# Split queries and keys of the attention: DMAs moved from GpSimd's software queue to SyncE's hardware queue

## The chip, the cores and the metric

One core of a Trainium2 chip runs the whole program. The metric is the device time of one execution in microseconds (us). The engines are TensorE (PE, with its weight loads as PEld), VectorE (DVE), ScalarE (ACT), GpSimd (POOL) and SyncE (SP), which only issues DMAs. Each engine takes its instructions in one fixed order; an instruction that waits holds all that stand behind it on its engine. A DMA issued by SP goes into the hardware queue (q1 in the profile), one issued by POOL into the software queue (q0); the data of both move through the core's 16 DMA engines.

## The reference

Two layers of a transformer-like block work on 1024 latent and 256 context tokens of width 1024. In each layer a normed and modulated input is projected into four mixers of 256 columns each: an mLSTM in both directions, a differential attention, a multiscale pool, and a gated convolution. Their outputs go together through one projection with a residual, and then through a SwiGLU feed forward with a residual. The attention has 4 heads, each with two maps of head width 32:

```
q = rms_norm(aq.reshape(B, L, 4, 2, 32), q_norm_g);  k = rms_norm(ak..., k_norm_g)
q, k = apply_axial_rope(q), apply_axial_rope(k)        # latent tokens only
s = einsum('bqhmd,bkhmd->bhmqk', q, k) * 32 ** -0.5;   p = softmax(s)
a = p[:, :, 0] - lam * p[:, :, 1];                     o = einsum('bhqk,bkhe->bqhe', a, v)
```

Latent queries see all 1280 keys, context queries the 256 context keys. The second layer needs no context output. All is float32; the gains are large, so products are made nearly exact by splitting the operands.

## The kernel before

Activations lie with features on partitions and tokens along the free dimension. A dense product is made of three float32r products, of the high and low parts of both operands (`mm3`, lines 274 to 279). Weights come as 256 KB tiles by SP (`load_w`, line 267), ACT copies out the high part and DVE or POOL subtracts the low part; there are two buffers for the raw tile (`wor`, `wfr` and so on in the profile) and five each for high and low.

A layer runs so: projections for mLSTM, convolution and pool; the mLSTM's states; then chunk after chunk of the mLSTM's outputs, with the projections of the attention's queries and keys, of its values, and the steps of the convolution's norm put between them as a filling (`background`); then the attention; the output projection (`out_proj`); the feed forward (`ffn`).

The queries and keys pass through DRAM. `qk_in` (lines 914 to 940) norms and rotates one projected tile of 128 features (4 maps of 32) by up to 512 tokens, writes its high part (ACT, into the buffer `qr`) and its low part (POOL, into `qsq`), and stores both in the scratch `qks`, laid out as [kind, map, high or low, 32 rows, 1280 tokens] (lines 939 and 940). `stacks(h)` (lines 1132 to 1145) loads them for one head: for each of its two maps, a tile `Qs` whose rows 0 to 63 hold the high part twice and rows 64 to 127 the low part twice (two DMAs of 64 rows), and a tile `Ks` with the high and low part, twice over (one DMA of 128 rows). The doubling is the leading [0, 2] of the source's access pattern (`dup`, lines 1126 and 1127), so that one product with 128 rows makes all four partial products. A head's six DMAs are Qs, Qs, Ks, Qs, Qs, Ks. In layer 0 a row has 1280 floats (320 KB a `Qs` DMA, 640 KB a `Ks` DMA); in layer 1 a `Qs` row has 1024 (256 KB). `stacks(0)` stands before the first score tile, and `stacks(1)`, `(2)`, `(3)` two slots after the start of the first, second and third head's scores; a slot is one score tile. The values come by SP from another scratch (`V`, line 1144).

The order on each engine is made by a planner ahead of the run, from a simulated time, from the order of the text as priority, and from free buffers. Only PE, ACT and DVE are held to the order of the text, and only inside the attention (`ordered`, class `Engine`). A DMA of either queue has one of eight semaphores for that queue in turn, so the ninth waits until the first has landed. A buffer is reused when the last one that reads it is done; for a store that is its landing. The tiles `T` (520 columns, 11 buffers) hold among others `yct` and `so` (outputs of convolution and mLSTM on their way to the scratch `ys`, lines 1109 and 911), `so` as loaded from the scratch `os` (line 904), `csq`, `qr` and `qsq`. The tiles `S` (28 buffers) hold `Qs`, `Ks`, the activations and the large work arrays.

In `out_proj` each weight's low part is ordered behind the last DMA of `stacks(3)` in the plan (`self.stack`, lines 1140 and 1332; `after`, lines 229 to 232, which orders without a wait). `woh` on ACT and `wol` on POOL thus stand inside the attention's last head.

Of the kernel before, what the change touches and what calls it, by code (L numbers as in the profile page):

```python
# [11 lines left out]
F32 = mybir.dt.float32  # L12
F32R = mybir.dt.float32r
BF16 = mybir.dt.bfloat16
AF = mybir.ActivationFunctionType
# [3 lines left out]
P = 128  # L19
# [21 lines left out]
# parameter columns of one layer  # L41
# [112 lines left out]
class Engine:  # L154
    """an engine whose instructions keep the order they are written in while builder.ordered is set"""
# [28 lines left out]
class Builder:  # L184
# [24 lines left out]
    # PSUM banks of each phase: for the dense products, for all else  # L209
# [19 lines left out]
    def after(self, ins, gate):  # L229
        """order ins behind gate in the schedule, without a wait"""  # L230
        self.tc.add_manual_dep(ins.ins, gate.ins.name, mybir.DependencyInfo(
            mybir.DependencyClass.NoSync, mybir.DependencyReason.DATA), reason="load order")
# [5 lines left out]
    def cb(self, name, n):  # L238
        """a constant column repeated n times"""
        return self.c(name)[:, 0:1].to_broadcast([P, n])  # L240
# [21 lines left out]
    def load_w(self, ap, n, eng=None, nm="w", gate=None):  # L262
        """weights [P, n] from DRAM as an exact sum of two float32r tiles"""
        hi = self.wp.tile([P, 544], F32R, tag="wh", name=f"{nm}h", bufs=5)
        lo = self.wp.tile([P, 544], F32R, tag="wl", name=f"{nm}l", bufs=5)
        raw = self.wp.tile([P, 544], F32, tag="wr", name=f"{nm}r", bufs=2)
        self.load = self.nc.sync.dma_start(raw[:, :n], ap)
        self.copy(hi[:, :n], raw[:, :n])
        ins = self.sub_lo(lo[:, :n], raw[:, :n], hi[:, :n], eng)
        if gate is not None:  # L270
            self.after(ins, gate)
        return hi, lo
# [12 lines left out]
    def rsqrt_steps(self, y, ms, eps, l=None):  # L285
        """y = (ms + eps) ** -0.5 with l for scratch; ms may be in PSUM"""
        nc = self.nc
        n = y.shape[-1]
        if l is None:
            l = self.T("rsl")[:, :n] if n > 64 else self.Q("rslq", n)  # L290
        epsc = self.eps[eps]
        nc.scalar.activation(l, ms, AF.Ln, bias=epsc)
        nc.scalar.activation(y, l, AF.Exp, scale=-0.5)
        yield
        nc.vector.scalar_tensor_tensor(l, ms, epsc, y, ALU.add, ALU.mult)
        nc.vector.scalar_tensor_tensor(l, l, -0.5, y, ALU.mult, ALU.mult)
        nc.vector.scalar_tensor_tensor(y, l, 1.5, y, ALU.add, ALU.mult)

    def sigmoid(self, out, x, n, t=None):
        """exp(min(x, 0) - log(1 + exp(-|x|))) with t for scratch"""  # L300
        nc = self.nc
        t = self.T("sgm")[:, :n] if t is None else t
        for _ in self.sigmoid_steps(out, x, t):
            pass
# [12 lines left out]
    def setup(self):  # L317
# [22 lines left out]
        # silu of the conditioning vectors, split  # L340
# [11 lines left out]
        # lambda of each layer  # L352
# [29 lines left out]
    def mod_steps(self, l, quads):  # L382
        """columns of (lat, ctx) modulation; each group of four 512 chunks runs on four column tiles"""
# [29 lines left out]
    def mod_vec(self, l):  # L413
        """all columns of (lat, ctx) modulation, two 512 chunks at a time: products and sums over the tiles of c on
        the vector engine, sums over partitions on the tensor engine; in steps of one vector instruction"""
# [32 lines left out]
    def norm_r(self, h, c0, n):  # L448
        """1 / rms of every token, on all partitions"""
        nc = self.nc  # L450
        px = self.PX("nps")
        for k in range(KT):
            sq = self.T("nsq")
            v = h[k][:, c0:c0 + n]
            nc.scalar.activation(sq[:, :n], v, AF.Square)
            g = slice((k % 4) * 32, (k % 4) * 32 + 32)
            nc.tensor.matmul(px[g, :n], self.cb("one", 32), sq[:, :n], start=(k < 4), stop=(k >= 4))
            if k == KT // 2 - 1:
                yield
        sm = self.T("nsum")[:, :n]  # L460
        self.copy(sm, px[:, :n])
        px = self.PX("nps2")
        nc.tensor.matmul(px[:, :n], self.cb("comb", P), sm, start=True, stop=True)
        r = self.T("nrstd")[:, :n]
        self.rsqrt(r, px[:, :n], 1e-6, sm)
        return r
# [8 lines left out]
    def norm_in(self, h, chunks):  # L475
        """the first norm: normalised in place, before the modulation is there"""
# [6 lines left out]
    def norm_mod(self, l, gname, sh, sc):  # L483
        """the split tiles of u, and what fills a chunk of them from h"""
# [39 lines left out]
    def fm_gen(self, l, idx, u, chunks, consume, src="w_fm", eng=None):  # L524
        """one 128 column tile, features on partitions"""
# [17 lines left out]
    def tm_gen(self, aps, n, u, cs, consume, w=None):  # L543
        """n columns, tokens on partitions"""
# [16 lines left out]
    def mixers(self, l, u, norm):  # L561
        """norm: what is left of the norm, in steps"""
# [7 lines left out]
        self.oc = range(0 if need else 2, NCH)      # token chunks whose outputs are needed  # L570
# [7 lines left out]
        # mLSTM: v with a ones column, gates  # L578
# [115 lines left out]
    def mix(self, a, n, b):  # L694
        """n steps of a, then steps of a and b in turn"""
# [10 lines left out]
    def mlstm_rows(self, Z):  # L706
# [11 lines left out]
        # log sigmoid of the forget gates  # L718
# [34 lines left out]
        nc.vector.tensor_scalar(mp[:, 1:2], am[:, 0:1], mp[:, 0:1], -1.0, ALU.max, ALU.mult)   # -Glast  # L753
        nc.scalar.activation(mp[:, 2:3], mp[:, 1:2], AF.Exp, bias=mp[:, 0:1])                  # e_old
# [19 lines left out]
        # -max(m, running max) of every row, spread block diagonally over the heads, as an exact sum of two  # L774
# [58 lines left out]
    def mlstm_chunk(self, c, kT, qT, Cst):  # L833
        """stages of the outputs of one chunk"""
# [79 lines left out]
    def qk_in(self, kind, i, c0, n, ps):  # L914
# [24 lines left out]
        nc.gpsimd.dma_start(self.qk_scr[kind, 4 * i:4 * i + 4, 0, :, c0:c0 + n], hi)  # L939
        nc.gpsimd.dma_start(self.qk_scr[kind, 4 * i:4 * i + 4, 1, :, c0:c0 + n], lo)  # L940
# [21 lines left out]
    def pool(self, u, i):  # L962
# [14 lines left out]
        for (o, c0, n) in segs:  # L977
            g = nc.gpsimd.tensor_tensor
            b = o + 8                       # column of token 0
            sw = s[:, o:o + n + 16]  # L980
            uw = up[:, o:o + n + 16]
            # column j of sw/uw is token j - 8
            if i == 0:
                g(sw[:, 7:n + 10], uw[:, 6:n + 9], uw[:, 7:n + 10], ALU.add)            # windows of 2
                x = self.S("psx")
                g(x[64:P, 8:n + 8], sw[64:P, 7:n + 7], sw[64:P, 9:n + 9], ALU.add)      # windows of 4
                res = ((0, 64, s, b), (64, P, x, 8))
            else:
                x = self.S("psx")
                g(sw[:, 1:n + 16], uw[:, 0:n + 15], uw[:, 1:n + 16], ALU.add)           # 2  # L990
                g(x[:, 2:n + 15], sw[:, 1:n + 14], sw[:, 3:n + 16], ALU.add)            # 4
                g(sw[:, 4:n + 13], x[:, 2:n + 11], x[:, 6:n + 15], ALU.add)             # 8
                g(x[64:P, 8:n + 8], sw[64:P, 4:n + 4], sw[64:P, 12:n + 12], ALU.add)    # 16
# [23 lines left out]
    def conv_in(self, u, i, cy):  # L1017
        """gated inputs: ctx tokens at column 0, latent tokens at column 271, zeros between"""
# [16 lines left out]
    def conv_taps(self, cy, acc):  # L1035
        """one tap of each half at a time, the middle one first"""
# [17 lines left out]
    def conv(self, acc):  # L1054
        """layer norm, silu and pointwise product, in steps; what is left of the last ones goes into the attention"""
# [64 lines left out]
    def attention(self):  # L1120
# [3 lines left out]
        gd = nc.gpsimd.dma_start  # L1124
# [7 lines left out]
        def stacks(h):  # L1132
            Qs, Ks = [], []
            for m in range(2):
                mp = 2 * h + m
                Qm = self.S(f"Qs{m}", F32R)
                gd(Qm[0:64, q0:NT], dup(self.qk_scr[0, mp, 0, :, q0:NT]))
                gd(Qm[64:P, q0:NT], dup(self.qk_scr[0, mp, 1, :, q0:NT]))
                Km = self.S(f"Ks{m}", F32R)
                self.stack = gd(Km[:, 0:NT], dup(self.qk_scr[1, mp].rearrange("a r n -> (a r) n")))  # L1140
# [6 lines left out]
        def scores(h, b0, nk, at):  # L1147
            """exp of both maps combined, unscaled: p0 - (lam * L0 / L1) * p1; two steps for each score tile"""
# [23 lines left out]
        def shared():  # L1172
            """one bank for both uses of a slot"""
# [15 lines left out]
        def weights_t(at, nk, aT):  # L1189
            """the combined weights with keys on partitions; a step for each two key tiles"""  # L1190
# [19 lines left out]
        def values(h, b0, nk, aT):  # L1210
            """the two query blocks on two column tiles; two steps of products, then the move out of PSUM"""
# [15 lines left out]
        def subln(pair, b0):  # L1227
            """norm over each head, with tokens on partitions for the statistics; the sums of the first map undo
            the missing scale of eps"""
# [32 lines left out]
        # four slots of a score tile each for a unit; its transposes and products some slots later  # L1262
# [4 lines left out]
        for i, (h, b0, nk) in enumerate(units):  # L1267
# [9 lines left out]
            d = {1: 4, 2: 1}.get(left, 0)        # the last ones earlier  # L1277
# [8 lines left out]
        rest = {1: 2, 2: 1, 3: 1, 4: 2, 5: 2}      # steps of what is left of the convolution, by slot  # L1286
# [174 lines left out]
def _layout(x, c, ctx, c_ctx, norm1_g, norm2_g, mod_w, mod_b, w_in, mlstm_gate_b, mlstm_norm_g,  # L1461
# [31 lines left out]
    # [l, chunk, k pair, 128, 2 k, 512]  # L1493
    o["mod_w"] = mod_w.reshape(L, 4, 2, P, 12, 512).transpose(0, 4, 1, 3, 2, 5).reshape(L, 12, 4, P, 1024)
    order = [(0, 256), (256, 512), (1040, 1296), (1296, 1552), (1808, 2064), (2064, 2320), (2320, 2576)]
    fm = np.concatenate([w_in[:, :, s:e] for s, e in order], axis=2)         # 14 tiles
    # [l, tile, piece, 128, 4 k, 128]
# [44 lines left out]
```

## Time and profile before

| | us |
|---|---|
| three timed runs | 3360.95, 3363.9, 3366.14 (median 3363.9) |
| profiled execution, span from first to last instruction | 3361.6 |
| PE busy in the span | 3099.8 (92%) |
| DVE, ACT, POOL busy | 1805.3, 1130.7, 520.9 |
| attention of layer 0, first score product to the fourth head's last units | 572 to about 790 |
| attention of layer 1 | about 2320 to 2500 |

PE is busy nearly everywhere but in the two attentions and just ahead of them; there its busy share falls to 5 to 8 tenths in the slices of the page. POOL's DMA issues stand in its own time line (about 0.7 us each), SP's in that of its queue ("SPq"). In the time line a row is: start, duration, engine, line, operation, what it writes and reads, shape, count, and in brackets the idle time of the engine before it and what ended it.

### The profile page before, as it was taken

The page shows a single profiled execution, that of the slowest core. Times are in us where ns is not written, and L with a number is a line of the kernel's source. Part 1 is how long each engine was busy: PE and PEld are TensorE (multiplying, and loading weights), DVE is VectorE, ACT ScalarE, POOL GpSimd, SP SyncE. Part 2 cuts the span into 40 slices and gives each one's busy share as a digit, 9 for nine tenths or more (in the row PEclk, how much of TensorE's full clock was granted, in tenths as well). Part 3 has the DMA queues.
Part 4 walks back from the last instruction along what each step waited for, and adds up shares of the span by engine and source line. Part 5 has one row for each costly group of instructions (what it writes and reads, how often), then busy time and mean ns, then how long its engine had stood idle before and what let it go on. Part 6 is the DMA issues. An engine that isn't in the chain of part 4 may idle for free. (4 is left out here: it accounts for less than half of the span.)

```text
span 3361.6 us, 41928 instructions
## 1 busy us (share of the span) xinstructions
PE 3099.8 (92%) x16504; PEld 2459.5 (73%) x16504; DVE 1805.3 (54%) x2868; ACT 1130.7 (34%) x2233; POOL 520.9 (15%) x412
## 2 busy tenths in 40 slices
PE   7999886778999999999999898985789999999999
PEld 3766664557778888888888686764667788888887
DVE  6494555875365555455433668566873533343343
ACT  4212444766441111111111622444874411111111
POOL 2240321232400000000000333321424000000000
PEclk9999987989999999999999998998999999999999
DMA  7123335223222222222111211344422111111112
GB/s 275 54 68 103 92 90 102 45 49 129 76 70 75 69 79 73 69 71 79 43 38 38 75 45 47 83 98 93 78 92 80 55 44 47 51 48 46 45 54 76
DMA packets 180566, 247.44 MB, mean 74 GB/s; under 512 B 70032, under 2 KB 82192, under 8 KB 180368
## 3 DMA queue, kind: packets, MB, share of 16 engines
q1 hardware_dynamic: 123600, 214.68, 20.3%
q0 software_dynamic: 56768, 30.07, 5.2%
q8 instruction: 130, 2.13, 0.3%
q14 instruction: 68, 0.56, 0.1%
HBM read 214.10 MB, written 30.41 MB: 73 GB/s over the span
## 5 line engine op out<-in xcount | busy, mean ns | idle before, releaser
L164 DVE SCALAR_TENSOR_TENSOR h<-xps,mod,h 128x512 f32<-128x512 f32 (+1 forms) x440 | 302.9, 697 | 187.1 <-PE xps L164 182.7
L164 PE MATMUL fps<-uh,wgh 128*128 128x512 f32 (+1 forms) x880 | 329.6, 375 | 6.1 <-ACT fsg L164 6.1
L164 PE MATMUL fps<-ul,wgh 128*128 128x512 f32 (+1 forms) x880 | 328.5, 373 | 0.6 <-DVE ul L164 0.6
L164 PE MATMUL fps<-uh,wgl 128*128 128x512 f32 (+1 forms) x880 | 328.4, 373 | 0.0
L164 PE MATMUL xps<-gl,wxh 128*128 128x512 f32 (+1 forms) x880 | 327.9, 373 | 0.0
L164 PE MATMUL fps<-uh,wuh 128*128 128x512 f32 (+1 forms) x880 | 327.3, 372 | 0.0
L164 PE MATMUL xps<-gh,wxl 128*128 128x512 f32 (+1 forms) x880 | 327.0, 372 | 0.0
L164 PE MATMUL fps<-uh,wul 128*128 128x512 f32 (+1 forms) x880 | 326.8, 371 | 0.0
L164 PE MATMUL fps<-ul,wuh 128*128 128x512 f32 (+1 forms) x880 | 326.8, 371 | 0.0
L164 PE MATMUL xps<-gh,wxh 128*128 128x512 f32 (+1 forms) x880 | 326.5, 373 | 0.0
L164 DVE TENSOR_TENSOR fsg<-fsg,fps 128x512 f32<-128x512 f32 (+1 forms) x110 | 69.7, 634 | 421.9 <-PE fps L164 419.5
L164 PE MATMUL fmps<-uh,wfh 128*128 128x512 f32 (+1 forms) x592 | 222.8, 376 | 13.7 <-ACT kT L164 13.7
L164 PE MATMUL fmps<-ul,wfh 128*128 128x512 f32 (+1 forms) x592 | 221.3, 374 | 0.0
L164 PE MATMUL fmps<-uh,wfl 128*128 128x512 f32 (+1 forms) x592 | 221.0, 373 | 0.0
L164 DVE TENSOR_REDUCE ls<-sc 128x1 f32<-128x1280 f32 (+1 forms) x144 | 195.0, 1367 | 32.1 <-PE sc L164 31.6
L164 PE MATMUL sc<-Ks,Qs 128*128 128x512 f32 (+1 forms) x400 | 124.4, 419 | 85.6 <-ACT pr L164 83.8
L164 DVE SCALAR_TENSOR_TENSOR acc<-cy,par,acc 128x1286 f32<-128x1286 f32 (+28 forms) x120 | 199.7, 1702 | 1.0
L164 PEld LDWEIGHTS fps<-uh,wgh 128*128 128x128 f32 x880 | 165.9, 189 | 44.7 <-ACT fsg L164 6.3
L164 PEld LDWEIGHTS fps<-ul,wgh 128*128 128x128 f32 x880 | 166.0, 189 | 36.4 <-DVE ul L164 2.6
L164 PEld LDWEIGHTS xps<-gh,wxh 128*128 128x128 f32 x880 | 165.5, 188 | 35.3 <-issue 3.1
L164 PEld LDWEIGHTS xps<-gl,wxh 128*128 128x128 f32 x880 | 165.3, 188 | 34.6 <-DVE gl L164 3.0
L164 PEld LDWEIGHTS fps<-uh,wgl 128*128 128x128 f32 x880 | 166.0, 189 | 32.4 <-issue 1.1
(286 smaller groups left out, 6130.4 us busy)
## 6 DMA issues: line engine op xcount, KB each, us to landing
mw<-in_mod_w SPq DMA_DIRECT2D x160, 256.0 KB, 3.9
wgr<-in_ffn_in SPq DMA_DIRECT2D x88, 256.0 KB, 2.6
wur<-in_ffn_in SPq DMA_DIRECT2D x88, 256.0 KB, 2.6
wxr<-in_ffn_out SPq DMA_DIRECT2D x88, 256.0 KB, 2.6
wor<-in_w_out SPq DMA_DIRECT2D x64, 256.0 KB, 2.7
wfr<-in_w_fm SPq DMA_DIRECT2D x56, 256.0 KB, 2.6
h<-in_xT SPq DMA_DIRECT2D x16, 640.0 KB, 6.8
Ks<-qks POOLq DMA_DIRECT2D x16, 640.0 KB, 26.2
```

The lines of the kernel that those rows point to most:

```text
L164: ins = f(*args, **kw)
```

## The change

The stores of `qk_in` and the loads of `stacks` are issued by SP instead of POOL. Both sides of each are now declared float32 instead of float32r (the same bits). The shapes, the sizes, the number and the order in the text stay. In the listing below only these edits are shown; elsewhere the diff takes out comments and docstrings.

```diff
@@ qk_in
-        nc.gpsimd.dma_start(self.qk_scr[kind, 4 * i:4 * i + 4, 0, :, c0:c0 + n], hi)
-        nc.gpsimd.dma_start(self.qk_scr[kind, 4 * i:4 * i + 4, 1, :, c0:c0 + n], lo)
+        for x, v in enumerate((hi, lo)):
+            nc.sync.dma_start(self.qk_scr[kind, 4 * i:4 * i + 4, x, :, c0:c0 + n].bitcast(F32), v.bitcast(F32))
@@ attention
-        gd = nc.gpsimd.dma_start
+        gd = nc.sync.dma_start
@@ stacks
-                gd(Qm[0:64, q0:NT], dup(self.qk_scr[0, mp, 0, :, q0:NT]))
-                gd(Qm[64:P, q0:NT], dup(self.qk_scr[0, mp, 1, :, q0:NT]))
+                for x in range(2):
+                    gd(Qm[x * 64:x * 64 + 64, q0:NT].bitcast(F32), dup(self.qk_scr[0, mp, x, :, q0:NT].bitcast(F32)))
                 Km = self.S(f"Ks{m}", F32R)
-                self.stack = gd(Km[:, 0:NT], dup(self.qk_scr[1, mp].rearrange("a r n -> (a r) n")))
+                self.stack = gd(Km[:, 0:NT].bitcast(F32),
+                                dup(self.qk_scr[1, mp].rearrange("a r n -> (a r) n").bitcast(F32)))
```

## Rows read from the trace of the kernel before

**Rows 1.** The page's first lines: busy time, share of the span, instructions.

```profile
span 3361.6 us, 41928 instructions
PE 3099.8 (92%) x16504; PEld 2459.5 (73%) x16504; DVE 1805.3 (54%) x2868; ACT 1130.7 (34%) x2233; POOL 520.9 (15%) x412
```

**Rows 2.** DMA issues: names, queue, count, KB each, median us to landing.

```profile
wor<-in_w_out SPq DMA_DIRECT2D x64, 256.0 KB, 2.7
Ks<-qks POOLq DMA_DIRECT2D x16, 640.0 KB, 26.2
Qs<-qks POOLq DMA_DIRECT2D x16, 320.0 KB, 21.9
qks<-qr POOLq DMA_DIRECT2D x16, 256.0 KB, 7.2
...
V<-vs SPq DMA_DIRECT2D x8, 320.0 KB, 2.9
```

**Rows 3.** DMA view, 2325 to 2333 us: GB/s by slice; queue: packets, MB, share of 16 engines.

```profile
GB/s 55 1 55 28 55 52 52 54 54 54 54 54 54 28 52 28 54 52 54 54 54 54 54 54 54 28 52 28 54 52 54 54 54 54 31 45 45 29 27 1
q0 software_dynamic: 67, 0.34, 11.0%
```

**Rows 4.** The same view, 787 to 797 us, where two `yr` loads of 640 KB run.

```profile
DMA packets 820, 3.75 MB, mean 375 GB/s; under 512 B 91, under 2 KB 91, under 8 KB 818
```

**Rows 5.** Time line of the way into layer 0's attention.

```profile
536.91 0.70 POOL L1137 DMA_DIRECT2D Qs<-qks  x1
...
542.48 1.56 SPq L1109 DMA_DIRECT2D ys<-yct  x2
...
542.82 0.74 POOL L1138 DMA_DIRECT2D Qs<-qks  x1
...
553.89 0.78 POOL L1140 DMA_DIRECT2D Ks<-qks  x1 [10.33 <-DMA Qs<-qks]
...
559.54 0.32 SPq L904 DMA_DIRECT2D so<-os  x1
...
562.82 0.63 ACT L164 ACTIVATE csq<-acc 128x512 f32<-128x512 f32 x1 [13.07 <-DMA ys<-yct]
...
570.49 0.42 DVE L164 TENSOR_TENSOR hs<-hs,so 128x256 f32<-128x256 f32 x1 [4.60 <-DMA so<-os]
...
572.28 2.50 PE L164 MATMUL sc<-Ks,Qs 128*128 128x512 f32 x6 [0.56 <-ACT so L164]
```

**Rows 6.** Time line of the same place in layer 1.

```profile
2282.11 0.70 POOL L1137 DMA_DIRECT2D Qs<-qks  x1
...
2310.25 0.63 ACT L164 ACTIVATE csq<-acc 128x512 f32<-128x512 f32 x1 [6.89 <-DMA ys<-yct]
...
2314.98 0.43 DVE L164 TENSOR_TENSOR hs<-hs,so 128x256 f32<-128x256 f32 x1 [2.56 <-DMA so<-os]
```

**Rows 7.** Time lines of POOL, SP and ACT: third and fourth head's loads, next weights.

```profile
624.86 0.68 POOL L1137 DMA_DIRECT2D Qs<-qks  x1
...
673.13 0.69 POOL L1137 DMA_DIRECT2D Qs<-qks  x1
...
678.68 25.19 SPq L267 DMA_DIRECT2D wor<-in_w_out  x5
...
699.20 0.63 ACT L164 ACTIVATE woh<-wor 128x512 fp32r<-128x512 f32 x1 [5.77 <-DMA wor<-in_w_out]
...
2366.50 0.68 POOL L1137 DMA_DIRECT2D Qs<-qks  x1
...
2406.11 0.69 POOL L1137 DMA_DIRECT2D Qs<-qks  x1
...
2427.67 0.63 ACT L164 ACTIVATE woh<-wor 128x512 fp32r<-128x512 f32 x1 [0.87 <-DMA wor<-in_w_out]
```

**Rows 8.** ACT's waits, 340 to 500 us: total us, times, longest.

```profile
ACT W L164 <- DMA qks<-qr: 9.9, 4, 4.8
...
ACT W L164 <- DMA qks<-qsq: 4.3, 2, 2.3
```

## The prediction

> **What bounds the kernel now.** I read the page first: PE is busy 92% of 3361.6 us [rows 1], so a change pays only where PE stands still. The slices of the page put that into the two attentions and just ahead of them, where the moved DMAs are. Then I read the time line there. In layer 0 POOL issues eight of the twelve loads of the first two heads between 536.91 and 542.82, and the rest from 553.89 on [rows 5]. SP issues two stores of `yct` at 542.48. ACT's `csq` needs one of their buffers and waits 13.07 us for the landing, to 562.82; the load of `so` also starts only at 559.54, and `hs`, the last step of the mLSTM, waits for it to 570.49. The first score product follows at 572.28. So what ends last before the attention is a chain of small transfers of the hardware queue, held up while the large loads use the DMA engines. Layer 1 shows the same: loads from 2282.11, `csq` at 2310.25, `hs` at 2314.98 [rows 6].
>
> The second such place is the fourth head. Its loads go out at 673.13; the first of five weight loads `wor` follows at 678.68, and ACT, whose order has two `woh` between the softmaxes, reaches the second at 699.20 after waiting for its weights [rows 7]. In layer 1 the second `woh` is at 2427.67.
>
> Within the attention ACT and DVE set the pace; a head's loads are asked for about 50 us ahead of use (624.86 to 673.13; in layer 1 2366.50 to 2406.11, 40 us).
>
> **How fast one load is.** This carries the forecast. From 2325 to 2333 one `Ks` load is nearly alone: slices show 54 GB/s, and the queue's packets fill 11.0% of 16 engines, 1.8 of them [rows 3]. A load of plain 128 rows in the hardware queue reaches 375 GB/s over two loads [rows 4]. So one load with the doubled source runs on about two engines at some 27 GB/s each, and not on sixteen. The change leaves its shape alone. The software queue makes up for this by running the loads side by side: a head's 2.6 MB (four of 328 KB, two of 655 KB) land within 26.2 us [rows 2], 100 GB/s, which one pair could not carry.
>
> What the hardware queue does with such a load no row shows. From below: it spreads over 16 engines, like `V` (320 KB in 2.9 us [rows 2]), 7 us for a head. In the middle: each load gets another pair, 26 us as now. From above: all loads lie on one pair, one behind the other. I take the last, because shape is what the trace ties to the two engines, and because taking turns is shown for the software queue alone, whose name says that a program fills it. At 54 GB/s a head then costs 4 x 6.1 + 2 x 12.1 = 48.5 us in layer 0, and 4 x 4.9 + 24.2 = 43.7 us in layer 1.
>
> The Trainium skill (page "DMA: Bandwidth & Descriptors", section "Why a DMA increments its semaphore by 16 and not by 1") speaks against this change: the number of engines is the largest up to 16 that divides the outermost dimension of both sides, so a source that begins with a repeat of two gets two, in either queue; the software queue then moves on from pair to pair, the hardware queue always takes the lowest-numbered. The 1.8 engines [rows 3] agree with the first half; the second half no run here shows yet; by the rule the sum is the one worked out below. By the same page's "Issuing engine by pattern", plain copies are generally faster from SP, and the sum would be that of the first rival below.
>
> **The change part by part.** I take it that the hardware queue serves each engine in order, so that whatever SP issues behind such loads and spreads over all 16 engines waits on that pair for them.
>
> (1) Into the attention, layer 0. I expect SP's plan to have the order of rows 5 merged: eight loads (head 0 and the first query tile of head 1), then the stores of `yct`, then `so`. The pair starts some 2 us after 536.91 and has the eight loads done at 539 + 48.5 + 12.2 = 600. The `yct` stores land behind them, at about 601 (now 562.8, when `csq` starts). `so` needs a buffer that they free, and lands some 2.5 us later, at 603.5. `hs` moves from 570.5 to 604: +34. With it move everything that follows on PE. Layer 1: 2284 + 43.7 + 9.8 = 2337.5, `so` at 2341.5 against 2315: +27. The eighth DMA in flight bounds SP too, but its waits end inside this time. Bounds: if only the first map's three loads are ahead of the stores, the second map's keys are late instead, +11 and +9; if all twelve are ahead, 97 and 87 us of loads, +70 and +61.
>
> (2) The fourth head. The third head's loads (624.86) fill the pair to 624.86 + 2 + 48.5 = 675.4, the fourth's to 723.9. `wor` is planned behind them and lands at about 726 (2.7 us alone [rows 2]); the second `woh` moves from 699.2 to 726.5: +27. ACT holds the softmaxes behind it, and all engines of the attention with them. Layer 1: 2366.5 + 2 + 43.7 = 2412.2, then 2455.9, `woh` at 2458 against 2427.7: +30 (this contains some 4 us by which the third head's last keys are late). Bounds: 0 if `wor` is planned ahead of the loads; a gain of 5.8 and 0.9, the waits in the brackets, if they also run freely.
>
> (3) The other heads: 48.5 against 48.3 us from 624.86 to 673.13 in layer 0, so nothing; the `V` loads queue behind head 1's last four loads and land about when they are used. If that cover goes, each microsecond counts.
>
> (4) The stores. 22 pairs leave POOL for SP. Landing takes 7.2 us now [rows 2], and ACT waits 9.9 + 4.3 = 14.2 us in layer 0 for buffers that they hold [rows 8]; a store's target begins with four maps, so I estimate four engines of 27 GB/s, 2.4 us and some 2 us of issue and landing for the high part, 2.4 more for the low one. That is 1 to 3 us less per store. Against that, SP now stands at a store until ACT and POOL have written it, and behind it are the rope tables, the next projection's weights and `so`. I take -5 a layer, between -14 (all of these waits) and +15 (the rope and weight loads late by 1.5 us for each of some ten pairs a layer).
>
> (5) POOL loses 92 issues at about 0.7 us (0.70 and 0.74 [rows 5]), 65 us of its 520.9 [rows 1]; it idles more than it works and gains nothing that PE waits for. SP takes about 0.35 us for each (0.32 [rows 5]), and has time.
>
> Sum: 34 + 27 + 27 + 30 - 5 - 5 = +108. The profiled execution's span is 3361.6; the median of the runs is 3363.9, 2.3 above it, and I set that on top: 3361.6 + 2.3 + 108 = 3472, say 3470.
>
> **Rivals.**
> *Spread over 16 engines: faster.* For it: every hardware load in the rows does so. Against it: the shape of rows 3. The crossing then loses its held-up stores: `csq` at 550 instead of 562.8 and `hs` about 15 us earlier, 12 in layer 1; `wor` lands in 2.7 us, -5.8 and -0.9; the stores -5 each. 3363.9 - 15 - 12 - 7 - 10 = 3320. It decides from the point where a head's loads take under some 20 us.
> *Pairs in turn.* Landings as now, `wor` behind the loads instead of beside them, a few us; the stores' gain against it: 3360 to 3370.
> *All twelve loads ahead of the stores.* For it: they stand in one block on POOL. Against it: those from 553.89 on wait for buffers, not only for a semaphore, so the planner should have seen `so` earlier. 70 + 61 + 57 - 10 = +178: 3542.
> *One pair, but slower.* With six loads at once each gets 100 / 6 = 17 GB/s now; at half of 54 the heads cost 97 us, load bound throughout: over +250, 3620. Alone in the queue I see no reason for it.
>
> **How the numbers follow.** Forecast 0.68, all twelve ahead 0.14, slower pair 0.03, spread 0.10, in turn 0.05. Likeliest time 3470; its own range, from its terms' bounds taken half way, is 3420 to 3520. The range 3385 to 3580 leaves out the spread case, the turns and the slow pair, under 2 in 10. A change below 0.2%, 7 us, can't be told from none. Faster 0.10; the same 0.04 (most of the turns); slower 0.86.
>
> **What would show it.** Right: `Ks` and `Qs` under the hardware queue land 12 to 60 us after issue, in steps along the queue; 50 to 55 GB/s and about 12% of 16 engines for tens of us around 540 to 600 and again under the third and fourth heads; `csq` and `hs` wait over 30 us for `yct` and `so`; `woh` waits over 30 us for `wor`. Wrong: loads that land in under 10 us, or a GB/s line near 300 there, mean the spread; landings near 25 us mean turns. If the total is near 3470 but (1) has twice its size and (2) none, the plan's order was misread.

## The result, and the profile after

| | before | after |
|---|---|---|
| median of the runs made side by side, us | 3365.02 (3360.95 to 3366.58) | 3491.52 (3490.57 to 3495.82) |
| ratio, 95% interval | | 1.0382 [1.0367, 1.0396] |
| span of the profiled execution, us | 3361.6 | 3494.0 |

The change costs 126.5 us; the forecast was +108, 3470 us. The page of the kernel after, as in [rows 1], and its queues:

```profile
span 3494.0 us, 41912 instructions
PE 3116.1 (89%) x16504; PEld 2472.2 (71%) x16504; DVE 1793.4 (51%) x2868; ACT 1131.4 (32%) x2233; POOL 464.0 (13%) x320
...
q1 hardware_dynamic: 133600, 244.56, 21.8%
```

Against [rows 1] PE is idle 116 us more, and busy 16 us more for the same 16504 products: its mean granted clock is 0.944 of full speed (2.4 GHz), against 0.965 before. The software queue is gone. Where the 132.4 us of the profiled span arose is read from the time lines, from marks that both kernels have (us):

| stage, up to | layer 0: before, after | longer by | layer 1: before, after | longer by |
|---|---|---|---|---|
| last tile of queries and keys (`qms` on PE) | 466.1, 476.3 | 10.2 | 2231.8, 2301.5 | 11.0 |
| first score product | 572.3, 582.2 | -0.3 | 2320.0, 2394.8 | 5.1 |
| second head's | 625.7, 648.2 | 12.6 | 2364.7, 2446.6 | 7.1 |
| third head's | 675.3, 698.5 | 0.7 | 2404.6, 2499.9 | 13.4 |
| fourth head's (the third head's scores, with `woh`) | 737.7, 798.1 | 37.2 | 2453.8, 2589.3 | 40.2 |
| first product of `out_proj` | 803.1, 864.1 | 0.6 | 2519.9, 2654.3 | -1.1 |

A stage runs from the mark above it to its own, and "longer by" is its own growth; the first row of layer 0 counts from the start of the span, and 1.8 of its 10.2 us arose ahead of the first `qms` (349.8, 351.6). So `woh` stands inside the third head's scores, while the fourth head's loads run, and not inside the last head, as "The kernel before" says. Layer 1 began 58.7 us late, which is taken off its first row (2191.2 against 2132.5 for the first `qms`). The two layers grow by 61.0 and 75.7; the feed forwards give 4.3 back.

**The pair.** The DMA view of the kernel after, 690 to 735 us, beside [rows 3]: GB/s by slice, then the queue's packets, MB, share of 16 engines, and what was issued meanwhile.

```profile
GB/s 55 50 55 50 55 50 55 55 50 67 52 50 36 55 46 55 55 55 46 55 55 55 46 55 55 55 50 50 55 55 50 50 55 55 50 55 50 55 55 55
...
q1 hardware_dynamic: 478, 2.35, 12.7%
...
Ks<-qks SPq DMA_DIRECT2D x2, 640.0 KB
Qs<-qks SPq DMA_DIRECT2D x3, 320.0 KB
```

12.7% of 16 engines is 2.0 engines. Before, one load alone ran on two; now five are issued in the stretch and together still run on two, at 52 GB/s; the trace's packets run two at a time for 43.4 of these 45 us. So in the hardware queue all doubled loads share one pair. In layer 0 it has work from the first of them to about 755. The same view from 536 to 640 us shows no slice under 41 GB/s, and from 736 to 766 us its low level ends only about 755:

```profile
GB/s 69 41 43 41 59 126 164 83 49 52 134 61 53 53 51 53 51 51 99 156 51 53 51 52 53 51 53 51 53 51 59 51 53 51 53 53 56 74 217 139
```

```profile
GB/s 55 55 48 55 184 296 152 249 87 280 74 55 55 55 48 48 55 55 55 48 48 55 51 53 46 25 25 11 0 0 0 183 167 0 22 0 98 262 186 153
```

In the second line the bytes of `V` and of the first `wor` loads that lie on other engines pass at 739 to 744 us; then only the pair moves, for 11 us, and ACT waits for the rest of `wor` behind it. A queue that finished one transfer before it began the next would not show this: only the share that lies on the pair waits.

**The fourth head's loads.** Time lines of SP and ACT in the kernel after, beside [rows 7]:

```profile
641.97 3.27 SPq L1138 DMA_DIRECT2D Qs<-qks  x2
...
713.30 13.05 SPq L1140 DMA_DIRECT2D Ks<-qks  x1
726.40 12.11 SPq L1145 DMA_DIRECT2D V<-vs  x1
738.60 25.15 SPq L267 DMA_DIRECT2D wor<-in_w_out  x5
```

```profile
756.47 0.63 ACT L164 ACTIVATE woh<-wor 128x512 fp32r<-128x512 f32 x1 [42.44 <-DMA wor<-in_w_out]
...
2554.89 0.63 ACT L164 ACTIVATE woh<-wor 128x512 fp32r<-128x512 f32 x1 [38.20 <-DMA wor<-in_w_out]
```

The waits of 690 to 800 us (total, times, longest) show what stands behind this one ACT instruction:

```profile
PEld sc L164 <- ACT pr L164: 51.7, 11, 43.3
PE sc L164 <- ACT pr L164: 49.8, 9, 43.2
POOL wol L260 <- ACT woh L164: 43.2, 2, 42.2
DVE ls L164 <- ACT pr L164: 43.2, 3, 42.3
ACT woh L164 <- DMA wor<-in_w_out: 42.4, 1, 42.4
```

**Into the attention**, beside [rows 5]: SP, ACT, DVE and PE, then layer 1 [rows 6] and the second map of its first head.

```profile
535.85 0.56 SPq L1138 DMA_DIRECT2D Qs<-qks  x1
545.35 0.35 SPq L653 DMA_DIRECT2D vs<-avt  x1
545.76 0.53 SPq L1138 DMA_DIRECT2D Qs<-qks  x1
550.08 0.82 SPq L1109 DMA_DIRECT2D ys<-yct  x2
...
553.76 0.51 SPq L1140 DMA_DIRECT2D Ks<-qks  x1
554.36 3.98 SPq L1138 DMA_DIRECT2D Qs<-qks  x1
558.44 3.64 SPq L904 DMA_DIRECT2D so<-os  x1
...
565.11 10.74 SPq L1140 DMA_DIRECT2D Ks<-qks  x1
```

```profile
559.51 1.14 ACT L164 ACTIVATE csq<-acc 128x512 f32<-128x512 f32 x2
```

```profile
579.10 0.43 DVE L164 TENSOR_TENSOR hs<-hs,so 128x256 f32<-128x256 f32 x1 [18.66 <-DMA so<-os]
```

```profile
582.21 1.43 PE L164 MATMUL sc<-Ks,Qs 128*128 128x512 f32 x3 [1.87 <-DVE csq L164]
598.46 1.83 PE L164 MATMUL sc<-Ks,Qs 128*128 128x512 f32 x4 [14.82 <-issue]
```

```profile
2388.38 0.42 DVE L164 TENSOR_TENSOR hs<-hs,so 128x256 f32<-128x256 f32 x1 [12.57 <-DMA so<-os]
```

```profile
2406.97 2.47 PE L164 MATMUL sc<-Ks,Qs 128*128 128x512 f32 x6 [11.33 <-DMA Ks<-qks]
```

The planner put the stores of `yct` behind two doubled loads and `so` behind four, not eight. `csq` no longer waits for such a store and starts 3 us sooner than before (559.51 against 562.82 [rows 5]). `hs` waits 18.66 us for it, but this is 8.6 us later than before (579.10 against 570.49 [rows 5]), no more than the store stage had already lost. PE's next wait is that for the second map's keys, 14.8 us. The bracket calls it "issue"; in layer 1 the same place is named as Ks, 11.33 us.

**The store stage.** Waits in 350 to 480 us of the kernel after: one line of POOL's, one of SP's queue.

```profile
POOL gq L933 <- DMA ropec<-in_rope: 36.9, 5, 9.7
```

```profile
SPq L940 <- ACT qr L164: 39.0, 7, 10.1
```

SP waits 39 us at stores, and POOL 36.9 us for rope tables; before, POOL waited for them once here, 8.6 us.

### The profile page after: what moved, and what is told of

The parts are those of the page before. It is cut to its first block, busy times and chain, and to the rows that moved or that the text cites. A ratio compares the mean times of both kernels' runs of the same rounds, so it can differ in the third digit from the quotient of the medians.

```text
span 3494.0 us, 41912 instructions
## 1 busy us (share of the span) xinstructions
PE 3116.1 (89%) x16504; PEld 2472.2 (71%) x16504; DVE 1793.4 (51%) x2868; ACT 1131.4 (32%) x2233; POOL 464.0 (13%) x320
## 5 line engine op out<-in xcount | busy, mean ns | idle before, releaser
L164 PEld LDWEIGHTS sc<-Ks,Qs 128*128 128x128 f32 x400 | 75.8, 217 | 182.8 <-ACT pr L164 124.6
L164 ACT ACTIVATE pr<-sc,ls 128x1280 f32<-128x1280 f32 (+1 forms) x144 | 178.5, 1240 | 50.6 <-DVE ls L164 49.4
```

The source lines that it names most:

```text
L164: ins = f(*args, **kw)
```

## The experiments

All were timed against the kernel before on the same chip (its medians: 3360.32 for e1 to e4, 3361.86 for e5 to e8, 3364.55 for e9 to e12; a difference between runs of two sets holds this shift of 1 to 4 us too). "All by SP" is the kernel after.

| run | stores | loads | median us | ratio to before [95%] |
|---|---|---|---|---|
| e1 | SP | POOL | 3388.69 | 1.0077 [1.0054, 1.0100] |
| e2 | POOL | SP | 3470.48 | 1.0323 [1.0299, 1.0346] |
| e3 | SP | SP, a DMA for each copy | 3342.90 | 0.9944 [0.9925, 0.9962] |
| e4 | SP | SP, `wor` by POOL | 3437.45 | 1.0225 [1.0202, 1.0247] |
| e5 | POOL | POOL, a DMA for each copy | 3319.52 | 0.9875 [0.9858, 0.9892] |
| e6 | SP, rope tables by POOL | POOL | 3374.36 | 1.0037 [1.0023, 1.0051] |
| e7 | POOL | SP, a DMA for each copy | 3317.65 | 0.9865 [0.9847, 0.9883] |
| e8 | SP | SP, repeat inside | 3333.84 | 0.9914 [0.9898, 0.9929] |
| e9 | POOL | SP, repeat inside | 3312.26 | 0.9844 [0.9826, 0.9863] |
| e10 | SP, rope tables and `so` by POOL | POOL | 3358.97 | 0.9990 [0.9975, 1.0006] |
| e11 | POOL, 128 rows | SP, repeat inside | 3265.60 | 0.9704 [0.9684, 0.9725] |
| e12 | SP, 128 rows | SP, repeat inside | 3273.18 | 0.9723 [0.9700, 0.9746] |

### Stores or loads alone (e1, e2)

```diff
# e1: the kernel after, but
-        gd = nc.sync.dma_start
+        gd = nc.gpsimd.dma_start
# e2: the kernel after, but
-            nc.sync.dma_start(self.qk_scr[kind, 4 * i:4 * i + 4, x, :, c0:c0 + n].bitcast(F32), v.bitcast(F32))
+            nc.gpsimd.dma_start(self.qk_scr[kind, 4 * i:4 * i + 4, x, :, c0:c0 + n].bitcast(F32), v.bitcast(F32))
```

> Only the stores of the split queries and keys go by SP; the loads stay on POOL. Theory (SP stands at a store until ACT and POOL have written it, and the rope tables and later loads behind it are late): the two store stages are about 10 us longer each, as in the changed kernel, so +20 us on the kernel before (3365), 3385. Rival (my prediction: stores land sooner and free their buffers, -5 a layer): 3355. Second rival (the longer store stage comes from the loads or from the plan as a whole): 3365.

> Only the loads of the split queries and keys go by SP; the stores stay on POOL. Theory: the loads carry what the stores don't, 126 - 20 = about +105 us, 3470, with the waits of woh for wor near 40 us in both layers' fourth heads. Rival (stores and loads collide only together in SP's queue): near 3400, with woh waits below 15 us.

e1 is 28.4 us slower than before and e2 110.2; together 138.6 against 126.5 for both at once. The stores lose, and the forecast's -5 a layer had the wrong sign. In e1 POOL waits 36.6 us for rope tables in 350 to 480 us, as in the kernel after. In e2 `woh` waits 43.06 and 38.18 us for `wor` in the two layers (42.44 and 38.20 in the kernel after): the loads do that alone.

### The shape of the loads (e3, e8), and the queue without it (e5, e7)

```diff
# e3, e5, e7: a DMA for each copy
-                    gd(Qm[x * 64:x * 64 + 64, q0:NT].bitcast(F32), dup(self.qk_scr[0, mp, x, :, q0:NT].bitcast(F32)))
+                    for y in range(2):
+                        o = x * 64 + y * 32
+                        gd(Qm[o:o + 32, q0:NT].bitcast(F32), self.qk_scr[0, mp, x, :, q0:NT].bitcast(F32))
-                self.stack = gd(Km[:, 0:NT].bitcast(F32),
-                                dup(self.qk_scr[1, mp].rearrange("a r n -> (a r) n").bitcast(F32)))
+                for y in range(2):
+                    self.stack = gd(Km[y * 64:y * 64 + 64, 0:NT].bitcast(F32),
+                                    self.qk_scr[1, mp].rearrange("a r n -> (a r) n").bitcast(F32))
# e8: the repeat behind the rows; each row stands twice in turn
+        def rep(ap):
+            r, n = (list(x) for x in ap.ap)
+            return AP(tensor=ap.tensor, offset=ap.offset, ap=[r, [0, 2], n])
+                    gd(Qm[x * 64:x * 64 + 64, q0:NT].bitcast(F32), rep(self.qk_scr[0, mp, x, :, q0:NT].bitcast(F32)))
+                for y in range(2):
+                    self.stack = gd(Km[y * 64:y * 64 + 64, 0:NT].bitcast(F32),
+                                    self.qk_scr[1, mp].rearrange("a r n -> r a n").bitcast(F32))
```

> The changed kernel with each copy of a doubled load as a DMA of its own: Qs as four of 32 rows for a map, Ks as two of 64 rows, the same bytes, all by SP, no leading repeat in the source. Theory (the repeat of two puts a load on two engines, always the same pair, and later transfers of the queue wait behind it): a head's loads land within some 10 us, woh waits under 6 us for wor, the crossing into the attention is shorter than before; what stays is the stores' loss: 3340 to 3385. Rival (the hardware queue is slow with these loads for another reason, as the scattered scratch, the number of DMAs or the order in SP): stays at 3470 to 3500.

> The changed kernel with the repeat kept in the source but not as its outermost dimension: Qs rows are written as row 0, row 0, row 1, row 1 and so on (source 32 rows, then the repeat of two), and Ks as two DMAs whose 64 rows run over row, then high or low; the product sums the same pairs in another order. Theory (the outermost count decides the number of engines, the repeat itself is free): as the third run, 3343 within 8 us, with half as many Qs DMAs. Rival (reading a row twice in one DMA is what is slow): 3430 to 3490.

> The kernel before (loads and stores by POOL), with each copy of a doubled load as a DMA of its own, as in the third run: the shape alone, in the software queue. Theory (the shape costs in either queue; the software queue only hides it by running loads side by side): the crossings and the woh waits gain about as in the third run, without the stores' loss: 3343 - 25 = about 3320, up to 3335 for POOL's 48 further issues. Rival (in the software queue the shape is hidden and costs nothing): 3360.

> The third run with the stores back on POOL: loads by SP, one DMA for each copy. Theory (the gain of the loads and the loss of the stores add): 3343 - 25 = about 3318, at most 3330. Rival (they don't add, since the order in SP changes as a whole): 3335 to 3350.

All four came out as the theory had it, but that e8 is 9 us below e3 and not within 8. A repeat behind the rows costs no more than separate copies; the same repeat ahead of them puts the load on two engines. The DMA view of e8, 610 to 640 us, shows a whole head's loads and its `V`, at about 200 to 290 GB/s and done in some 13 us:

```profile
GB/s 0 0 0 89 294 266 232 219 225 246 239 259 219 225 219 250 212 239 198 253 58 3 0 11 22 0 0 0 0 0 0 0 0 0 0 0 0 0 0 0
```

In e3 the first `woh` of layer 0 no longer waits:

```profile
682.40 0.62 ACT L164 ACTIVATE woh<-wor 128x512 fp32r<-128x512 f32 x1
```

e5 and e7 differ in the loads' queue alone, and by 1.9 us, less than can be told apart. So with the doubled shape the hardware queue costs the loads 110 us (e2), and with a plain shape nothing. The change's sign lies in the shape.

### Another queue for the late weights (e4)

```diff
-                w = [self.load_w(self.a["w_out"][l, nt, pc], 512, nc.gpsimd, "wo", self.stack) for pc in range(2)]
+                w = [self.load_w(self.a["w_out"][l, nt, pc], 512, nc.gpsimd, "wo", self.stack, nc.gpsimd) for pc in range(2)]
```

> The changed kernel with the weight loads of the output projection (wor) issued by POOL into the software queue; the doubled loads stay in the hardware queue. Theory (wor is late because it waits its turn behind the loads in the same queue): woh's waits fall from 42.4 and 38.2 us to under 10, 50 to 75 us less than the changed kernel (3491), 3415 to 3440. Rival (the busy pair of engines itself is the limit, whichever queue asks): woh still waits 20 us or more, 3470 to 3491.

54 us less than the kernel after; the longest wait of a `woh` for `wor` inside the attention is now 4.2 us in layer 0 and 2.4 in layer 1. The pair is still full, but `wor` now lands in 6.2 us (DMA view of e4, 700 to 717 us: the burst over 300 GB/s is `wor`'s, and the queue's line counts its packets):

```profile
GB/s 48 48 72 48 48 48 87 82 100 308 421 366 84 67 57 43 55 47 43 65 48 48 48 60 48 60 48 48 48 60 48 60 48 48 60 48 48 60 48 48
...
q0 software_dynamic: 160, 0.52, 9.3%
...
wor<-in_w_out POOLq DMA_DIRECT2D x2, 256.0 KB, 6.2
```

The orders of PE and DVE are those of the kernel after, instruction for instruction. So `wor` was late because it stood in the same queue behind the loads; the pair serves another queue beside it, if more slowly than alone (2.7 us in the kernel before [rows 2]). The Trainium skill (page "DMA: Bandwidth & Descriptors", section "Queues, rings and completion order") says that each engine takes packets from its queues in turn, with which this agrees.

### Why the stores lose (e6, e10, e12), and what their shape costs (e11 against e9)

```diff
# e6: e1 with
-            nc.sync.dma_start(cs, self.a["rope"][:, 0, t])
-            nc.sync.dma_start(sn, self.a["rope"][:, 1, t])
+            nc.gpsimd.dma_start(cs, self.a["rope"][:, 0, t])
+            nc.gpsimd.dma_start(sn, self.a["rope"][:, 1, t])
# e10: e6 with
-        nc.sync.dma_start(so, self.o_scr[c])
+        nc.gpsimd.dma_start(so, self.o_scr[c])
# e9: e8 with the stores by POOL
# e11: e9, and e12: e8, with another order of the scratch
-        self.qk_scr = self.dp.tile([2, 8, 2, 32, NT], F32R, name=f"qks{l}")
+        self.qk_scr = self.dp.tile([2, 2, 8, 32, NT], F32R, name=f"qks{l}")
# the stores' target, and Qs's and Ks's source
-    self.qk_scr[kind, 4 * i:4 * i + 4, x, :, c0:c0 + n]
+    self.qk_scr[kind, x, 4 * i:4 * i + 4, :, c0:c0 + n].rearrange("m r n -> (m r) n")
-    self.qk_scr[0, mp, x, :, q0:NT]
+    self.qk_scr[0, x, mp, :, q0:NT]
-    self.qk_scr[1, mp].rearrange("a r n -> r a n")
+    self.qk_scr[1, :, mp].rearrange("a r n -> r a n")
```

> The first run (stores by SP, loads by POOL) with the rope tables' loads moved to POOL. Theory (of the loads held behind a waiting store, the rope tables are the ones that cost): gq's wait for ropec falls from 36.6 us in layer 0's stage to under 12, and the time from 3389 to 3360-3370. Rival (the weights and so held behind the stores cost it): 3380 to 3395.

> The sixth run (stores by SP, their rope tables by POOL, doubled loads by POOL) with the loads of so moved to POOL as well. Theory (what is left of the stores' loss, 14 us, is so held behind waiting stores; hs waits 14.3 us for it in layer 0's stage): 3360 to 3365, no loss left. Rival (it is the weights held behind the stores): 3370 to 3380.

e6 took back about half of the loss (28.4 us above its kernel before, then 12.5), where nearly all was expected. The wait for `ropec` fell to 10.2 us, and that of `hs` for `so` rose to 14.3. e10 moved `so` too: `hs` waits 4.4 us for it, and the loss is gone (0.9990, an interval that holds 1). So what stood behind the stores and cost time were the rope tables and `so`. No run moves these two with the stores left on POOL, so a gain from that move by itself isn't ruled out. The planner's order differs a little between these kernels, so how the loss splits between the two is less sure than the sum of both.

> The eighth run (repeat inside, loads by SP) with the stores back on POOL: the sum of what the runs showed. If the stores' loss adds as between the third and the seventh run (25 us): 3334 - 25 = 3309, faster than every kernel so far. If the gain of the eighth run over the third (9 us) came from fewer issues ahead of the stores in SP, and SP has none of them now: 3318, as the seventh.

> The ninth run with the scratch laid out as kind, high or low, map, so that a store's target is one run of 128 rows instead of four maps of 32. Theory (the store's outermost four puts it on four engines; on POOL nobody waits long for it): 0 to -8 us against the ninth run. Rival (a store is not limited by its engines): within 3 us of it.

> The eighth run (all by SP, repeat inside) with the stores' target in 128 rows, as in the eleventh. Theory (the stores' loss on SP is the wait of SP in its order, not the transfer): stays at 3334, within 6 us. Rival (stores on four engines hold up the rope tables and weights behind them in the queue): 3310 to 3320.

e9 at 3312 lies between the two sums, 3 us from the first and 6 from the second, which does not tell them apart for certain. e11 and e12 overthrew the theory on the stores: I had expected 0 to -8 and no change, and they are 46.7 us below e9 and 60.7 below e8. The order of PE, DVE and ACT is the same in e9 and e11, and in e8 and e12, so this is no other plan. Two stores of a pair in the hardware queue, in the DMA view: e8, 459 to 466 us, then e12, 454 to 459 us (GB/s by slice, share of 16 engines; the second burst of e12 has rope tables in it too):

```profile
GB/s 0 0 0 0 0 0 0 23 59 47 12 0 35 0 12 0 35 59 59 70 59 70 105 94 94 94 105 105 105 94 94 117 94 117 94 94 105 105 105 105
...
q1 hardware_dynamic: 206, 0.41, 20.4%
```

```profile
GB/s 0 0 0 0 0 0 0 0 0 0 0 246 377 393 393 360 312 17 0 0 0 0 279 344 393 377 426 279 230 197 164 197 131 33 0 16 82 0 16 66
...
q1 hardware_dynamic: 358, 0.67, 52.7%
```

With four maps outermost the stores run at about 105 GB/s, which four engines at some 26 each would give; with 128 rows at up to 393 (the first burst). On POOL the same can be read from the landing times: e9, then e11, 350 to 520 us.

```profile
ropec<-in_rope SPq DMA_DIRECT2D x8, 256.0 KB, 5.8
...
qks<-qr POOLq DMA_DIRECT2D x8, 256.0 KB, 7.2
qks<-qsq POOLq DMA_DIRECT2D x8, 256.0 KB, 9.8
...
wtr<-in_w_av SPq DMA_DIRECT2D x4, 256.0 KB, 5.4
```

```profile
ropec<-in_rope SPq DMA_DIRECT2D x8, 256.0 KB, 3.5
...
qks<-qr POOLq DMA_DIRECT2D x8, 256.0 KB, 2.4
qks<-qsq POOLq DMA_DIRECT2D x8, 256.0 KB, 2.6
...
wtr<-in_w_av SPq DMA_DIRECT2D x4, 256.0 KB, 2.7
```

The stores land in a third of the time, and most loads of the other queue that run beside them come sooner as well (`ropes`, 3.4 and 3.7 us, does not). With that shape SP for the stores costs 7.6 us (e12 against e11, whose runs spread over 11 and 7 us), with the old one 21.6 (e8 against e9) and 28.4 (e1). Most of the stores' loss is thus their transfer, on four engines ahead of the rope tables and `so` in one queue; the 7.6 us are what is left for SP standing in its order. The new layout also changes the addresses of the scratch, and no run separates that from the number of engines. The two views tell them apart: 0.41 MB in 7 us over 20.4% of 16 engines are 18 GB/s for each engine at work in e8, 0.67 MB in 5 us over 52.7% are 16 in e12. An engine is no slower at the old addresses; there are fewer of them.

e11, 3265.6 us, is the fastest, 2.96% below the kernel before, with the loads by the hardware queue, as the change wanted, and the loads and stores of queries and keys over many engines.

## Why the prediction was right, and where it was not

**One pair, one load behind another** (the claim that carried it): right. 52 GB/s against the 54 forecast, 2.0 engines with several loads issued. e3 and e8 take the shape away and the loss turns into a gain; e2 keeps it alone and has nearly all of the loss. The Trainium skill (page "DMA: Bandwidth & Descriptors", section "Why a DMA increments its semaphore by 16 and not by 1") gives both halves, and its second, that the hardware queue always takes the same engines, is now borne out too: 12.7% of 16 engines with five loads asked for. The same rule gives four engines for a target of four maps, and the 105 GB/s of the stores agree with it. By its "Issuing engine by pattern", plain copies are generally faster from SP; e5 and e7, 1.9 us apart, show no difference. For loads with the doubled source e2 shows 110 us the other way.

**(1) Into the attention**, +34 and +27: too large. Measured is +12.3 and +12.2 (first score product and first head together). The step that failed is the merged order, eight loads ahead of the stores of `yct` and of `so`. SP's plan has two of them ahead of the `yct` stores and four ahead of `so`. My lower bound, the second map's keys late instead, +11 and +9, is nearly what came. Of the signs, `csq` and `hs` were to wait over 30 us: `csq` came sooner than before, and `hs` waited 18.7 and 12.6. I had merged two queues by their times of issue; the planner ordered them anew.

**(2) The fourth head**, +27 and +30: right in place and cause (in the kernel after it is already the first of the stage's three `woh` that waits), too small in size; measured is +37.2 and +40.2. The step that failed is that the third head's loads fill the pair from 624.86 + 2 on, as if it were free. It was not free then: four heads of 2.6 MB at 52 GB/s are 202 us, and it was busy from about 536 to 753. So the backlog of the first two heads was carried into the fourth, and `woh` came at 756.47 where a pair that was free at 641.97 would have been done with two heads (2 x 50.4) at some 743. I had also read one wait too few: before the `woh` of [rows 7] stands another, in both layers, so that the waits already there were 10.6 and 5.6 us and not 5.8 and 0.9. The kernel before:

```profile
692.80 0.63 ACT L164 ACTIVATE woh<-wor 128x512 fp32r<-128x512 f32 x1 [4.87 <-DMA wor<-in_w_out]
...
2425.59 0.63 ACT L164 ACTIVATE woh<-wor 128x512 fp32r<-128x512 f32 x1 [4.71 <-DMA wor<-in_w_out]
```

**(3) The other heads**, 0: right in layer 0 (+0.7), wrong in layer 1 (+13.4, of which I had counted 4 under (2)). There a head's loads take 43.7 us by my own sum and the heads follow each other after 40 to 45, so the pair is the bound, and the backlog makes it worse; PE waits 10.3 us for Ks.

**(4) The stores**, -5 a layer: wrong sign, +10.2 and +11.0 in the store stage. The rate was estimated rightly (four engines of 27 GB/s), but I priced it as sooner landing for the buffers and not as some 5 us of queue for whatever comes next: two stores of 256 KB at 105 GB/s, ahead of rope tables and `so`. The upper bound, +15, named the mechanism with 1.5 us a pair, a third of that.

**(5) POOL's relief**, nothing: POOL's busy time falls by 57 us (520.9 to 464.0), and no stage above is shorter by more than 1.1 us.

That the total came within 18.5 us is in part luck: (1) and (2) to (4) were off in opposite directions. Measured less forecast, in the profiles: -36.5 for (1), +20.4 for (2), +14.1 for (3), +31.2 for (4), -0.5 in the last heads' ends, -4.3 in the feed forwards; 24.4 in all (132.4 against 108). The 132.4 hold the 16 us that PE itself was busy longer at its lower clock, a term that the forecast did not have: it took a change to pay only where PE stands still.

**The rivals.** "Spread over 16 engines" is nearly the account of e8, where all goes by SP in a plain shape: 3333.84, for 3320; what it had wrong is the stores, which lose 21.6 us there (e8 against e9) and do not gain 10, and the loads, which gain more than its 34 us (e9, with the stores on POOL, is 52.3 below its kernel before). "All twelve loads ahead" and "slower pair" did not occur. Several loads side by side, as in "pairs in turn", is what the software queue gives, and even there the shape was not free: e5 is 42 us below the kernel before, in the same queue.

## What to carry to other kernels

Before a DMA is moved to another queue, look at how many engines it runs on: its GB/s alone in a slice, and its share of 16 engines. Where the outermost count of one side is small (a repeat of two, four maps), the software queue hides a part of it by running transfers side by side (left were 42 us for the repeat, e5, and 47 for the four maps, e9 to e11), and the hardware queue hides none of that (110 us more for the repeat, e2, and 14 more for the four maps, e8 to e12): the transfer is late, and so is everything behind it in that queue, however small or differently shaped. Put the repeat behind the rows, or lay the scratch out so that 128 rows are outermost, and price a queue's narrow engines by their whole backlog, not head by head.

## What the runs showed that was not expected

- The stores' layout was worth 47 us (e9 to e11) and 61 us (e8 to e12), more than the choice of queue for anything but the doubled loads, though [rows 8] shows only 14.2 us of ACT's waits for their landing in layer 0. What they kept late is a part of it: `ropec` from 5.8 to 3.5 us, `wtr` from 5.4 to 2.7, besides their own 7 to 10 us.
- Another part is PE's clock. The profiled spans of e9 and e11 are 50.8 us apart, and 29.0 of these are PE's busy time (3095.4 against 3066.4 us) for the same products in the same order. Layer 0's store stage, first `qms` to last, in e9 and then e11 (from and to, length, busy us and count of PE, PEld, DVE, ACT and POOL, granted clock, share of the DMA engines, GB/s):

```profile
351.40:468.70 117.30, 103.51 (x507) 78.91 (x507) 70.66 (x141) 52.43 (x131) 44.05 (x45) 0.90 0.38 98
```

```profile
353.10:453.90 100.80, 93.13 (x507) 71.39 (x507) 72.03 (x143) 52.19 (x131) 42.20 (x45) 1.00 0.36 112
```

PE idles 6 us less here and is busy 10 us less. In e11 the upper level of the clock, 2.4 GHz, was granted throughout; in e9 it fell to 1.2 GHz four times in this stretch, some 24 us in all, each time just after PE had stood waiting. So a late transfer seems to cost twice here, once as the wait and once as a slower PE behind it; no run separates the two.
- A busy pair holds up another queue little. `wor` (256 KB over 16 engines) landed in 6.2 us by POOL with the pair full (e4), against 2.7 us in the kernel before [rows 2], where by SP `woh` had it 17.9 us after its first issue (738.60 to 756.47).
- A transfer over all engines behind narrow ones moves most of its bytes at once and then waits for the share of the busy ones: up to 296 GB/s at 739 to 744 us in the kernel after, then 11 us at about 50.
